# Four more seven-product units in a split-fp32 encoder kernel on one Trainium2 core

## The chip, the cores and the metric

The kernel runs on one core of one Trainium2 chip. The metric is the device time of one execution in microseconds (us), the median of several runs. The engines' names are those of the profile: PE is the matrix engine (matmuls), PEld its weight load, DVE the vector engine, ACT the scalar engine, POOL the GpSimd engine, SP the queue that issues the weight loads from the chip's memory.

## The reference, cut to what matters

Two layers of an encoder over 256 tokens of width 2048, all in fp32. Layer 0 mixes tokens by neighbourhood attention (16 heads of 128, one output projection of 2048 by 2048), layer 1 by a gated short convolution (an input projection to 6144, a three-tap convolution, an output projection of 2048 by 2048). Each layer is followed by a gated feed-forward block: an up-projection to 2 x 5632 columns, a three-tap convolution over positions, silu of one half times the other, and a down-projection back to 2048.

```python
h = h + mixed                                   # mixed = attention or short convolution, @ w_o / w_out
h = h + conv_glu_ffn(rms_norm(h, ffn_norm[i]), ffn_w_up[i], ffn_conv_w[i], ffn_conv_b[i], ffn_w_down[i])

def conv_glu_ffn(x, w_up, conv_w, conv_b, w_down):
    h = dwconv_centered(x @ w_up, conv_w) + conv_b
    g, u = jnp.split(h, 2, axis=-1)
    return (jax.nn.silu(g) * u) @ w_down
```

Each projection streams its weights from the chip's memory while PE works.

## The kernel before, in words

**Split fp32.** PE multiplies in a reduced format, so each fp32 operand x is held as a high part (ACT casts it, line L198 for weights, L318 for activations) and a low part (DVE subtracts, L201 and L319). A product costs three matmuls: high x high, high x low, low x high (function `product`, lines L480 to L482). In the up- and input projections (`Phase`, lines L279 and L287) the same sum is made in another arrangement of the operands.

**Projections back to the model width** are done by the class `Tokens`: the attention's output (called wo here), the four down-projections (two halves of the hidden width in each of two layers), and the convolution mixer's output. Each has two groups g of 1024 output columns. In a group four accumulators 11, 21, 12 and 22 (token half, column half; 128 tokens by 512 columns each, tile `mm`) are summed over pairs of 128-deep contraction blocks. The text of a plan such as `P0 P1 H5 P2 H6 P3 H7 P4` is the order of the pairs.

- A **P** pair has two weight chunks, left and right column half, 128x1024 each. It takes 2 blocks x 4 accumulators x 3 = 24 matmuls of 128x512.
- An **H** pair is done with seven block products in place of eight (`seven`): 7 x 3 = 21 matmuls. Four of the products go to four more accumulators (tile `mu`). It needs sums of weight blocks and sums of activation blocks. For each H pair and group (a "unit") four weight chunks are prepared: left (128x1024), w22 (128x512, split into hi and lo inside one tile), t13 and t42 (128x1024 each). Half of t42 is one more addition on DVE (L160). After the last H of a group, `combine` adds the `mu` accumulators into the residual stream `h`: one ACT copy (L514) and eight DVE operations of 128x512 (L515 to L522). The accumulators `mm` are added to `h` by `residual` (L377).

**Weight sums** are made in memory by DMA, far ahead: `make` issues three 256 KB copies per unit on ACT's DMA queue and three accumulating DMAs on POOL's queue into a buffer `kept`, which SP loads later (512 KB and 256 KB). The tuples QK_JOBS, V_JOBS, UP_JOBS and SC_JOBS say how many such jobs are issued in which earlier projection; the jobs run in the order in which the units are used.

**Activation sums** ("forms") are made by `make_forms`: four POOL operations of 128x128 (through `pool`, L233, which keeps POOL's work in program order), then a split into high (ACT) and low (DVE) parts. In the attention they are made in `mix`, which handles two heads at a time: ACT copies the pair's result out of PSUM (L686, tile `s`, two buffers), POOL makes the four sums in another `s` tile, ACT and DVE split them. `mix` for heads 12 and 13 and for heads 14 and 15 falls into the first items of wo.

**What sets the order.** The program is written item by item; before each item the chunks up to four further ones are loaded and split, `after(n, fn)` puts a function n items later, and a scheduler fixes each engine's order of instructions before the run. Each engine executes its list in order. Tiles come from rings: `raw`, `hi` and `lo` have six buffers each, `s` two, `a` 16 (first the attention's input, then the next layer's input), `act` 22.

At a **seam** (the end of one group and the start of the next) DVE has, in its list, the low parts of the last P pair and of the next group's first pair, `combine`, and the four residual additions. The first item of the next group writes accumulators 11 and then 21 again, six matmuls each, so it needs the old 11 and 21 added to `h` by then.

In the last down-projection the last two pairs are done by `finale`, which closes the accumulators one after the other so that the output can begin.

Of the kernel before, what the change touches and what calls it, by code (L numbers as in the profile page):

```python
# [15 lines left out]
F32 = mybir.dt.float32  # L16
# [6 lines left out]
P = 128  # L23
D = 2048
S = 256
KT = D // P
NH = 16
# [18 lines left out]
def plan(text, due):  # L46


    words = text.split()
    return (tuple(int(x[1:]) for x in words), {int(x[1:]): {"H": 3, "K": 4}[x[0]] for x in words if x[0] != "P"}, due)  # L50


S_FIRST = (plan("P0 H1 H3 H4 H5 P2 H6 H7 H8 H9 P10", 3), plan("P0 H1 H3 H4 H5 P2 H6 H7 H8 H9 P10", 6))
S_SECOND = plan("P0 P2 H1 H3 H4 P9 H5 H6 H7 H8 P10", 0)
S_MLP = {(0, 0): S_FIRST, (0, 1): (plan("P0 H1 H3 H4 H5 P2 H6 H7 H8 H9 P10", 0), plan("P0 P2 H9 H1 H3 H4 H5 H6 H7 H8 P10", 0)),
         (1, 0): S_FIRST, (1, 1): (S_SECOND, plan("P0 P2 H1 H3 H4 P5 H6 H7 H8 P9 P10", 0))}
S_OUT = (plan("P0 H1 H2 P3 H4 H5 H6 P7", 0), plan("P0 P3 H1 H2 H4 H5 H6 P7", 0))
S_ATT = (plan("P0 P1 H5 P2 H6 P3 H7 P4", 0),) * 2
QK_JOBS, V_JOBS, UP_JOBS, SC_JOBS = (0, 2, 2, 2), (2, 2, 2, 2), (12, 13, 11, 13), 14


HEAD = (2, 4)
# [18 lines left out]
def trunk(ctx, tc, xT, par, bias, wqk, wv, wo, wsc, wscout, wup, wdown, out):  # L81
    nc = tc.nc
# [3 lines left out]
    tp = ctx.enter_context(tc.tile_pool(name="tmp", bufs=2))  # L86
# [141 lines left out]
    def pool(op, **of):  # L228

        with ExitStack() as order:  # L230
            if "POOL" in newest:
                order.enter_context(tc.issue_after(newest["POOL"].ins))
            newest["POOL"] = op(**of)  # L233
# [64 lines left out]
    def after(n, fn):  # L298
        later.append((at[0] + n, fn))
# [33 lines left out]
    def a_tile():  # L333
        return ap_.tile([P, 2 * S], F32R, name="a", tag="a", bufs=KT)
# [204 lines left out]
    def make_forms(xe, xo, place, fresh=False):  # L539

        if fresh:
            form_at[:], left_over[:] = ("sf", "vv", "qk") * 2, ()
        v = tp.tile([P, 4, P], F32, name="s", tag="s")
        x11, x21, x12, x22 = (x[:, t * P:(t + 1) * P] for x in (xe, xo) for t in range(2))
        pool(nc.gpsimd.tensor_sub, out=v[:, 0, :], in0=x21, in1=x22)
        pool(nc.gpsimd.tensor_sub, out=v[:, 1, :], in0=v[:, 0, :], in1=x11)
        pool(nc.gpsimd.tensor_add, out=v[:, 3, :], in0=x12, in1=v[:, 1, :])
        pool(nc.gpsimd.tensor_sub, out=v[:, 2, :], in0=x11, in1=x21)
        if isinstance(place, tuple):
            hi, lo = place  # L550
            split_into(hi, lo, v.rearrange("p f c -> p (f c)"))
            return [(hi[:, j * P:(j + 1) * P], lo[:, j * P:(j + 1) * P]) for j in (0, 1, 3, 2)]

        blocks = 3 if place else 4
        y = form_slots(blocks)
        if isinstance(y, list):
            at = [(x[:, :P], x[:, P:]) for x in y]
            to = [(*at[j], v[:, j]) for j in range(blocks)]
        else:
            y = y.rearrange("p (b t c) -> p t b c", t=2, c=P)  # L560
            at = [(y[:, 0, j], y[:, 1, j]) for j in range(blocks)]
            to = [(y[:, 0, :blocks], y[:, 1, :blocks], v[:, :blocks])]
        if place:
            at.append((place[:, P:2 * P], place[:, 3 * P:]))
            to.append((*at[3], v[:, 3]))

        def splits():
            for x in to:
                split_into(*x)
        after(LATE, splits)  # L570
        return [at[j] for j in (0, 1, 3, 2)]
# [30 lines left out]
    oT = [None] * NH  # L602
    oforms = {}
# [66 lines left out]
    def mix(hs, v):  # L670

        o = pa.tile([P, 2, S], F32, name="o", tag="o")
        for i, h in enumerate(hs):
            for k in range(2):
                p = heads[h]["pT"][k]
                vh, vl = (x[:, h % 4 * P:(h % 4 + 1) * P] for x in v[k])
                nc.tensor.matmul(o[:, i, :], lhsT=vh, rhs=p[:, :S], start=k == 0, stop=False)
                nc.tensor.matmul(o[:, i, :], lhsT=vh, rhs=p[:, S:], start=False, stop=False)
                nc.tensor.matmul(o[:, i, :], lhsT=vl, rhs=p[:, :S], start=False, stop=k == 1)
        for i, h in enumerate(hs):  # L680
            oT[h] = act_tile()
            split(oT[h], o[:, i, :])
            heads[h].clear()
        if hs[0] // 2 in S_ATT[0][1]:
            x = tp.tile([P, 2, S], F32, name="s", tag="s")
            nc.scalar.copy(out=x, in_=o)  # L686

            place = tuple((a_tile if hs[0] // 4 == NH // 4 - 1 else act_tile)() for _ in range(2))
            oforms[hs[0] // 2] = make_forms(x[:, 0, :], x[:, 1, :], place)

    class Values:

# [40 lines left out]
    def sc_evac(f, ps):  # L733
# [11 lines left out]
        else:  # L745
# [3 lines left out]
            if j % 2 == 0:  # L749
                sc_of["even"] = t  # L750
            elif j // 2 in S_OUT[0][1]:
                yforms[j // 2] = make_forms(sc_of["even"], t, in_both(S_OUT, j // 2) and yT[j - 1], not yforms)

# [185 lines left out]
    for r in range(KT // STEP):  # L939
        for i in range(STEP // 2):  # L940
            k = r * STEP + 2 * i
# [101 lines left out]
```

## Time and profile before

| what | value |
|---|---|
| median of 3 runs | 2181.46 us (2181.4 to 2182.39) |
| the profiled execution's own time | 2181.86 us |
| its span (first to last instruction) | 2180.1 us |
| PE busy | 2170.2 us (100%), 11681 matmuls |
| DVE busy | 1768.3 us (81%) |
| ACT busy | 1329.0 us (61%) |
| POOL busy | 360.9 us (17%) |
| granted PE clock | 0.998 |
| moved by DMA | 582.61 MB, mean 267 GB/s |

A busy time is the union of an engine's instructions; matmuls overlap one another, so the distance between the starts of matmuls, and not the duration of one, is what a matmul costs. The stage boundaries in the trace: wo runs from 304 to 392 us, the convolution's output from 1373 to 1455 us, the last down-projection from 2055 to 2170 us.

### The profile page before, as it was taken

Reading aid. Unit: us, or ns where it says so; the run is one execution under the profiler, and the core shown is the slowest. Engines: PE = TensorE matmul, PEld = TensorE weight load, DVE = VectorE, ACT = ScalarE, POOL = GpSimd, SP = SyncE. Lnnn points to the kernel's source line nnn. Section 1 sums busy time; section 2 is a strip of 40 time slices with the busy share of each in tenths; the row PEclk is TensorE's granted clock in tenths of the full one; section 3 lists DMA queues with packets and bytes.
Section 4 is the critical chain, followed back from the end, with each engine's and each line's share of the span. In section 5 each row is a group of like instructions: output and inputs, shape, how many; then the busy total and the mean of one; then the engine's idle time right before and its main releaser. Section 6 shows DMA issues by size and latency. Waiting matters only on the chain.

```text
span 2180.1 us, 33378 instructions
## 1 busy us (share of the span) xinstructions
PE 2170.2 (100%) x11681; PEld 1882.8 (86%) x11681; DVE 1768.3 (81%) x2703; ACT 1329.0 (61%) x2032; POOL 360.9 (17%) x410
## 2 busy tenths in 40 slices
PE   9999999999999999999999999999999999999998
PEld 8888888888888888888888888888888888888887
DVE  8777668878789977779986676898788998788798
ACT  7555556665566666666764455666666666566565
POOL 0232130023220013230001323001222000232100
PEclk9999999999999999999999999999999999999999
DMA  8999997799998999999879999787999889999885
GB/s 282 280 280 252 263 222 251 226 278 261 279 262 281 313 257 291 291 258 276 271 241 263 291 302 272 256 270 217 281 288 258 268 286 289 286 269 285 234 273 184
DMA packets 451160, 582.61 MB, mean 267 GB/s; under 512 B 23344, under 2 KB 349616, under 8 KB 450992
## 3 DMA queue, kind: packets, MB, share of 16 engines
q1 hardware_dynamic: 235520, 458.84, 61.4%
q0 software_dynamic: 92400, 60.57, 20.7%
q10 hardware_dynamic: 123072, 61.07, 10.2%
q8 instruction: 92, 1.51, 0.3%
q14 instruction: 76, 0.62, 0.1%
HBM read 578.29 MB, written 123.21 MB: 322 GB/s over the span
## 4 chain that ended last, share of the span: by engine, by line
PE 98%; DVE 1%; ACT 0%; issue 0%; DMA 0%; SPq 0%; ACTq 0%; DVEq 0%
PE mm L279 43%; PE mm L287 22%; PE mm L480 6%; PE mm L481 6%; PE mm L482 6%; PE mu L481 3%; PE mu L480 3%; PE mu L482 3%; PE mm L712 1%; PE mm L713 1%; PE mm L714 1%; PE tr L388 1%; PE tr L665 0%; DMA raw<-in_wqk 0%; DVE lo L201 0%
## 5 line engine op out<-in xcount | busy, mean ns | idle before, releaser
L201 DVE TENSOR_TENSOR lo<-raw,hi 128x1024 fp32r<-128x1024 f32 (+1 forms) x869 | 1032.7, 1214 | 205.3 <-PE mm L287 135.0
L198 ACT CAST hi<-raw 128x1024 fp32r<-128x1024 f32 (+1 forms) x946 | 935.2, 1007 | 415.1 <-PE mm L279 105.1
L279 PE MATMUL mm<-a,hi 128*128 128x512 f32 x4096 | 961.9, 391 | 0.8 <-DVE a L327 0.5
L279 PEld LDWEIGHTS mm<-a,hi 128*128 128x128 f32 x4096 | 759.3, 188 | 154.3 <-DVE a L327 2.4
L287 PEld LDWEIGHTS mm<-a,lo 128*128 128x128 f32 x4096 | 512.9, 191 | 11.8
L287 PE MATMUL mm<-a,lo 128*128 128x256 f32 x4096 | 518.1, 283 | 0.0
L480 PE MATMUL mm<-hi,act 128*128 128x512 f32 x570 | 222.5, 390 | 0.0
L482 PE MATMUL mm<-hi,act 128*128 128x512 f32 x570 | 221.9, 390 | 0.0
L358 DVE SCALAR_TENSOR_TENSOR conv<-pad,pt,conv 128x256 f32<-128x256 f32 x384 | 184.1, 481 | 28.8 <-ACT conv L356 17.9
L233 POOL DMA_DIRECT2D kept<-in_wdown x122 | 163.3, 1918 | 262.0 <-DMA kept<-in_wdown 262.0
L356 ACT ACTIVATE conv<-pad,pt 128x256 f32<-128x256 f32 x176 | 105.7, 602 | 150.8 <-DVE pad L348 150.8
L481 PE MATMUL mm<-lo,act 128*128 128x512 f32 x498 | 194.0, 389 | 0.0
L342 ACT COPY corr<-mm 128x256 f32<-128x256 f32 x256 | 93.8, 370 | 134.9 <-PE mm L287 133.4
L233 POOL TENSOR_TENSOR s<-conv 128x128 f32<-128x128 f32 x62 | 31.5, 508 | 740.4 <-DVE conv L771 740.4
L480 PEld LDWEIGHTS mm<-hi,act 128*128 128x128 f32 x570 | 107.0, 188 | 22.3 <-DVE h L377 0.4
L482 PEld LDWEIGHTS mm<-hi,act 128*128 128x128 f32 x570 | 107.0, 188 | 22.2
L343 DVE TENSOR_TENSOR corr<-mm,corr 128x256 f32<-128x256 f32 x256 | 106.8, 418 | 22.7 <-ACT corr L342 22.7
L233 POOL DMA_DIRECT2D kept<-kept x77 | 80.4, 1047 | 199.0 <-DMA kept<-in_wdown 112.0
L481 PEld LDWEIGHTS mm<-lo,act 128*128 128x128 f32 x498 | 93.5, 188 | 18.8
L319 DVE TENSOR_TENSOR act<-conv,act 128x256 fp32r<-128x256 f32 x88 | 38.5, 438 | 68.3 <-ACT act L318 68.3
L480 PE MATMUL mu<-hi,sf 128*128 128x512 f32 x213 | 82.9, 389 | 0.0
L481 PE MATMUL mu<-lo,sf 128*128 128x512 f32 x213 | 82.9, 389 | 0.0
(160 smaller groups left out, 1723.7 us busy)
## 6 DMA issues: line engine op xcount, KB each, us to landing
raw<-in_wup SPq DMA_DIRECT2D x352, 512.0 KB, 6.4
raw<-in_wdown SPq DMA_DIRECT2D x115, 512.0 KB, 5.0
raw<-in_wsc SPq DMA_DIRECT2D x96, 512.0 KB, 6.8
kept<-in_wdown ACTq DMA_DIRECT2D x183, 256.0 KB, 6.4
raw<-kept SPq DMA_DIRECT2D x77, 512.0 KB, 5.3
kept<-in_wdown POOLq DMA_DIRECT2D x122, 256.0 KB, 12.0
raw<-in_wqk SPq DMA_DIRECT2D x56, 512.0 KB, 6.7
kept<-kept POOLq DMA_DIRECT2D x77, 256.0 KB, 10.6
```

The lines of the kernel that those rows point to most:

```text
L198: newest["ACT"] = nc.scalar.copy(out=hv, in_=r)
L201: newest["DVE"] = nc.vector.tensor_sub(out=lv, in0=r, in1=hv.bitcast(F32))
L233: newest["POOL"] = op(**of)
L279: nc.tensor.matmul(self.ps[ft], lhsT=prepped[i][0][:, o:o + P], rhs=self.src[k], start=k == 0, stop=False)
L287: nc.tensor.matmul(self.ps[ft][:, S:], lhsT=prepped[i][1][:, o:o + P], rhs=self.src[k][:, :S], start=False, stop=k == self.nk - 1)
L342: nc.scalar.copy(out=corr, in_=ps[:, S:])
L343: nc.vector.tensor_add(out=corr, in0=ps[:, :S], in1=corr)
L356: nc.scalar.activation(c, x[:, 1:S + 1], AF.Identity, scale=w[1], bias=b)
L358: nc.vector.scalar_tensor_tensor(out=c, in0=x[:, tap:tap + S], scalar=w[tap], in1=c, op0=ALU.mult, op1=ALU.add)
L480: nc.tensor.matmul(ps, lhsT=xh, rhs=wh, start=start, stop=False)
L481: nc.tensor.matmul(ps, lhsT=xh, rhs=wl, start=False, stop=False)
L482: nc.tensor.matmul(ps, lhsT=xl, rhs=wh, start=False, stop=stop)
```

## The change

Four units more are done with seven products: 81 in place of 77.

- wo: pair 4 becomes an H pair in both groups; the order is P0 P1 H5 P2 H6 H4 H7 P3.
- The convolution's output: pair 3 becomes H in the first group (six H pairs in a row); in the second it stays P.
- The last down-projection, second group: pair 5 becomes H (seven H pairs in a row, in the order of before).
- Pair 4's activation sums are not made from PSUM in its own `mix` but after the last `mix` (heads 14 and 15): two POOL additions of 128x256 restore heads 8 and 9 as high part plus low part, and `make_forms` then runs on these. Its parts lie in two `a` tiles.
- The weight-sum jobs are dealt out anew: 13, 13, 13, 14 in the four up-projections in place of 12, 13, 11, 13. The first of them in the attention now belong to wo's added units.

```diff
-         (1, 0): S_FIRST, (1, 1): (S_SECOND, plan("P0 P2 H1 H3 H4 P5 H6 H7 H8 P9 P10", 0))}
-S_OUT = (plan("P0 H1 H2 P3 H4 H5 H6 P7", 0), plan("P0 P3 H1 H2 H4 H5 H6 P7", 0))
-S_ATT = (plan("P0 P1 H5 P2 H6 P3 H7 P4", 0),) * 2
-QK_JOBS, V_JOBS, UP_JOBS, SC_JOBS = (0, 2, 2, 2), (2, 2, 2, 2), (12, 13, 11, 13), 14
+         (1, 0): S_FIRST, (1, 1): (S_SECOND, plan("P0 P2 H1 H3 H4 H5 H6 H7 H8 P9 P10", 0))}
+S_OUT = (plan("P0 H1 H2 H3 H4 H5 H6 P7", 0), plan("P0 P3 H1 H2 H4 H5 H6 P7", 0))
+S_ATT = (plan("P0 P1 H5 P2 H6 H4 H7 P3", 0),) * 2
+LATE_PAIRS = (4,)
+QK_JOBS, V_JOBS, UP_JOBS, SC_JOBS = (0, 2, 2, 2), (2, 2, 2, 2), (13, 13, 13, 14), 14
...
-        if hs[0] // 2 in S_ATT[0][1]:
+        if hs[0] // 2 in S_ATT[0][1] and hs[0] // 2 not in LATE_PAIRS:
             x = tp.tile([P, 2, S], F32, name="s", tag="s")
             nc.scalar.copy(out=x, in_=o)
 
             place = tuple((a_tile if hs[0] // 4 == NH // 4 - 1 else act_tile)() for _ in range(2))
             oforms[hs[0] // 2] = make_forms(x[:, 0, :], x[:, 1, :], place)
+        if hs[1] == NH - 1:
+            for i in LATE_PAIRS:
+                x = tp.tile([P, 2, S], F32, name="s", tag="s")
+                for k in range(2):
+                    hi, lo = (oT[2 * i + k][:, j:j + S].bitcast(F32) for j in (0, S))
+                    pool(nc.gpsimd.tensor_add, out=x[:, k, :], in0=hi, in1=lo)
+                oforms[i] = make_forms(x[:, 0, :], x[:, 1, :], tuple(a_tile() for _ in range(2)))
```

## The prediction

> **What bounds the kernel now.** I read the page first, then the groups of instructions, then the timelines of PE, DVE, ACT and POOL around wo and at the ends of the groups.
>
> ```profile
> span 2180.1 us, 33378 instructions
> PE 2170.2 (100%) x11681; PEld 1882.8 (86%) x11681; DVE 1768.3 (81%) x2703; ACT 1329.0 (61%) x2032; POOL 360.9 (17%) x410
> PE 98%; DVE 1%; ACT 0%; issue 0%; DMA 0%; SPq 0%; ACTq 0%; DVEq 0%
> L279 PE MATMUL mm<-a,hi 128*128 128x512 f32 x4096 | 961.9, 391 | 0.8 <-DVE a L327 0.5 <-ACT hi L198 0.2
> ```
>
> PE is busy all the time, the chain that ended last is PE's own to 98%, and the most frequent matmul waited 0.8 us in 4096 uses. So whatever takes matmuls away shortens the run by their spacing, as long as the other engines keep up. What a matmul costs is read from starts, not durations. PE's timeline in wo's first group, with the first matmuls of P3, H7 and P4 and two of the next group:
>
> ```profile
> 333.04 0.39 PE L480 MATMUL mm<-hi,act 128*128 128x512 f32 x1
> 338.48 0.39 PE L480 MATMUL mu<-hi,act 128*128 128x512 f32 x1
> 343.24 0.39 PE L480 MATMUL mm<-hi,act 128*128 128x512 f32 x1
> 348.68 0.39 PE L480 MATMUL mm<-hi,act 128*128 128x512 f32 x1
> 350.04 0.39 PE L480 MATMUL mm<-hi,act 128*128 128x512 f32 x1
> ```
>
> The P pair takes 338.48 - 333.04 = 5.44 us for 24 matmuls, the H pair 343.24 - 338.48 = 4.76 us for 21: both 0.227 us each. **An added unit saves 0.68 us of PE, four save 2.72 us.** That is 0.12% of the time; a measurement of this kernel can tell about 0.2% (4.4 us) from no change, so even the full gain lies below that.
>
> **What a unit asks of DVE.** H needs three subtractions of 128x1024, one of 128x512 and one addition; P needs two of 128x1024. DVE's timeline in a group with eight H pairs in a row (second half of layer 0, second group) shows one 128x512 subtraction per H pair; these are the second and the sixth of the row:
>
> ```profile
> 1065.39 0.69 DVE L201 TENSOR_TENSOR hi<-raw,hi 128x512 fp32r<-128x512 f32 x1
> 1085.15 0.68 DVE L201 TENSOR_TENSOR hi<-raw,hi 128x512 fp32r<-128x512 f32 x1
> ```
>
> Four pairs in 19.76 us is 4.94 us of DVE per H pair, against 4.76 us of PE. In a row of H pairs DVE falls behind by 0.18 us per pair. Two subtractions in succession take 2.28 us (lines starting 322.14 and 324.42 below), so a P pair gives DVE 5.44 - 2.28 = 3.16 us to catch up. **Turning P into H adds 4.94 - 2.28 = 2.66 us to DVE and takes 0.68 us from the time it has.** Where that ends late is at the seam: DVE has to run `combine` and the residual additions before PE reuses the accumulators. DVE in wo's first group, with its idle times:
>
> ```profile
> 321.19 0.69 DVE L319 TENSOR_TENSOR a<-s,a 128x512 fp32r<-128x512 f32 x1 [1.42 <-ACT a L318]
> 322.14 2.36 DVE L201 TENSOR_TENSOR lo<-raw,hi 128x1024 fp32r<-128x1024 f32 x2 [0.26 <-ACT hi L198]
> 324.42 0.68 DVE L201 TENSOR_TENSOR hi<-raw,hi 128x512 fp32r<-128x512 f32 x1
> ...
> 329.62 2.59 DVE L201 TENSOR_TENSOR lo<-raw,hi 128x1024 fp32r<-128x1024 f32 x2 [0.17 <-ACT hi L198]
> ...
> 334.52 2.36 DVE L201 TENSOR_TENSOR lo<-raw,hi 128x1024 fp32r<-128x1024 f32 x2 [0.99 <-ACT hi L198]
> 337.09 1.23 DVE L201 TENSOR_TENSOR lo<-raw,hi 128x1024 fp32r<-128x1024 f32 x1 [0.21 <-ACT hi L198]
> 339.81 1.23 DVE L201 TENSOR_TENSOR lo<-raw,hi 128x1024 fp32r<-128x1024 f32 x1 [1.50 <-ACT hi L198]
> ...
> 341.56 2.35 DVE L201 TENSOR_TENSOR lo<-raw,hi 128x1024 fp32r<-128x1024 f32 x2
> 343.83 0.68 DVE L515 TENSOR_TENSOR s<-mu,s 128x512 f32<-128x512 f32 x1
> ...
> 348.63 1.28 DVE L377 TENSOR_TENSOR h<-mm,h 128x512 f32<-128x512 f32 x2
> ```
>
> Idle from 322 us to the seam: 0.26 + 0.17 + 0.99 + 0.21 + 1.50 = 3.13 us. From 339.81 on DVE has no gap, and the second accumulator (the first of the two at 348.63, about 0.68 us long) is free at 349.31; PE writes it from 350.04. The margin is 0.73 us.
>
> **The change, part by part.**
>
> *wo, first group.* DVE gets 2.66 us for H4 and 0.62 us for splitting pair 4's sums (0.68, pipelined), and PE arrives 0.68 us earlier: 3.96 us, against 3.13 us of idle time. That leaves 0.83 us, 0.10 us over the margin. To this comes what POOL does to DVE. Pair 4's sums are two additions of 128x256, which the trace does not show, and four of 128x128. Their rows (minimum, median and maximum, ns), the two chains now run, and DVE's work beside the first of them:
>
> ```profile
> L233 POOL TENSOR_TENSOR bias<-bias,pt x16: 1012/1164/2973, 31.3 to 273.4; 128x384 f32<-128x384 f32 x16
> L233 POOL TENSOR_TENSOR s<-s x12: 452/462/1519, 248.1 to 320.1; 128x128 f32<-128x128 f32 x12
> ```
>
> ```profile
> 311.34 3.03 POOL L233 TENSOR_TENSOR s<-s 128x128 f32<-128x128 f32 x4 [25.40 <-ACT s L686]
> 312.40 1.23 DVE L201 TENSOR_TENSOR lo<-raw,hi 128x1024 fp32r<-128x1024 f32 x1 [1.76 <-ACT hi L198]
> 317.64 2.86 POOL L233 TENSOR_TENSOR s<-s 128x128 f32<-128x128 f32 x4 [3.28 <-ACT s L686]
> 318.54 1.23 DVE L201 TENSOR_TENSOR lo<-raw,hi 128x1024 fp32r<-128x1024 f32 x1 [1.60 <-ACT hi L198]
> 320.45 1.71 POOL L233 DMA_DIRECT2D kept<-kept x2
> ```
>
> A 128x256 addition lies between 0.46 us (128 columns) and 1.01 us (384); I take the middle, 0.73. Four operations of 0.46 would be 1.9 us; with a DVE subtraction beside them they take 3.03 and 2.86, and the longest operation, 1.52 us, is the shortest plus 1.07: POOL stood still while DVE subtracted. What DVE loses to POOL is bounded by nothing from below and by POOL's whole work from above: 2 x 0.73 + 4 x 0.46 = 3.3 us, less the first addition, which falls into DVE's idle 1.42 us before 321.19 (POOL is done with pair 7 at 317.64 + 2.86 = 320.5): 2.6 us. In the four forms above it was POOL that waited, not DVE, so I take the middle, 1.3 us. **The seam then costs 0.1 + 1.3 = 1.4 us, with ends 0.1 and 2.7.**
>
> The Trainium skill has a rule on this: in SBUF — State Buffer, Who interferes with whom, a DVE instruction with two SBUF inputs and a GpSimd instruction that reads SBUF exclude each other for a whole instruction, and whichever starts first keeps the port. The trace agrees, with the 1.52 us. By that rule the two engines' work adds up and the seam would cost up to the 2.7 us; without it 0.1. The same skill, GPSIMD Engine Reference, Elementwise, gives 4497 ns for an addition of 2048 columns, by which an estimate for 256 would be 0.56 us and the upper end 0.3 us lower.
>
> *wo, second group.* The same units without pair 4's sums. DVE is not held up by POOL there and starts the group further ahead; 0.1 us at most, I take 0.
>
> *Convolution output.* Six H in a row in the first group in place of three after a P: 3 x 0.18 = 0.5 us later at the seam. With wo's margin of 0.73 us, which I assume for it, that is 0; the upper end is 0.5. Pair 3's sums and split run in the input projection, under PE, with the five that are there already.
>
> *Last down-projection.* Seven H in a row in place of three after P5: 4 x 0.18 = 0.72 us later at its end, where the margin is small:
>
> ```profile
> 2162.23 1.28 DVE L377 TENSOR_TENSOR h<-mm,h 128x512 f32<-128x512 f32 x2
> 2163.03 0.60 PE L812 MATMUL tr<-pt,h 128*128 128x128 f32 x4
> ```
>
> The first of these additions ends at 2162.91 and PE transposes its result at 2163.03, 0.12 us later; behind the transposes stand PE's remaining matmuls. So 0.72 - 0.12 = 0.6; the ends are 0 (DVE may take the addition before `combine`) and 0.8. **I take 0.5 us.** If the cover were gone altogether, the seven pairs would cost what DVE needs more than PE, 1.3 us.
>
> *Jobs and loads.* Each unit adds three copies on ACT's DMA queue, three accumulating DMAs on POOL's and two loads on SP's:
>
> ```profile
> raw<-in_wup SPq DMA_DIRECT2D x352, 512.0 KB, 6.4
> raw<-in_wv SPq DMA_DIRECT2D x32, 512.0 KB, 4.7
> L198 ACT CAST hi<-raw 128x1024 fp32r<-128x1024 f32 (+1 forms) x946 | 935.2, 1007 | 415.1 <-PE mm L279 105.1 <-PE mm L482 79.8 <-DMA raw<-in_wup 33.1
> ```
>
> ACT waits mostly for PE, that is, for free buffers; its 33.1 us for up-projection weights have reached PE for none. I take 0. If a job held one weight load back by the difference of the medians, 1.7 us, and all of it reached PE, four would cost 6.8 us.
>
> **Sum.** -2.72 + 1.4 + 0.5 = -0.8 us on the profiled execution's 2181.86 us (span 2180.1 and 1.8 around it): 2181.0. The median of the runs is 0.4 us below that execution, so the forecast for the median is 2181.46 - 0.8 = **2180.7 us**.
>
> **The rivals.**
>
> *Everything is hidden.* Chance 0.26. If POOL slips its six operations into DVE's gaps and the last group's addition comes early, only 0.1 us is paid: 2181.46 - 2.72 + 0.1 = 2178.8. For it: 77 units run now with hardly a PE wait. Against it: DVE has no gap from 339.81 to the seam.
>
> *ACT's queue stops behind pair 4's split.* Chance 0.20, the one on the slower side. ACT runs its list in order:
>
> ```profile
> 314.40 0.62 ACT L318 CAST a<-s 128x512 fp32r<-128x512 f32 x1 [2.03 <-POOL s L233]
> 317.46 1.05 ACT L198 CAST hi<-raw 128x1024 fp32r<-128x1024 f32 x1
> 320.54 0.62 ACT L318 CAST a<-s 128x512 fp32r<-128x512 f32 x1 [2.03 <-POOL s L233]
> ```
>
> Both splits stand one weight cast behind the copy and hold ACT for 2.03 us. If pair 4's stands one cast behind pair 7's, ACT waits from 322.1 until POOL is through: 320.5 + 3.3 + DVE's 0.6 and 1.2 between = 325.6. The casts of H6 queue behind it, and DVE behind them. DVE then loses POOL's 2.6 us and 1.1 us more that it waits for the split and the first cast behind it: 0.1 + 3.7 = 3.8 at the seam, with the last group's 0.5: 4.3 - 2.72, 1.6 us slower, 2183.0. It decides from a stall of 2.2 us in wo on. Against it: casts of P2 and H6 may stand ahead of the split.
>
> *The DMA jobs reach PE.* Chance 0.05, 2181.46 - 0.8 + 6.8 = 2187.5. Against it speaks the 0.8 us in 4096.
>
> *Units without gain*, H4's sums so late that the pair itself waits: PE comes to H4 at 333.04 and the sums are there by 328 on the worst count above, so I give it 0.03, with a time like the ACT rival's.
>
> **How the numbers follow.** The forecast has 0.46. Its own range goes from 2179.4 to 2182.0 (seam 0.1 to 2.7). The range of 8 in 10 reaches to the hidden case and to the ACT rival: 2178.6 to 2183.2; left out are the DMA case and the ends. Faster by over 0.2% would need 4.4 us, more than all matmuls saved: 0.03. Slower by over 0.2% is the DMA case or several stalls together: 0.06. Within 0.2%: 0.91.
>
> **What would show it.** In the new profile 12 matmuls fewer; PE's distance between the first matmuls of H4 and H7 4.76 us. In wo's first group DVE without idle time from 322 us to the seam, and PE's first item of the second group, or the transposes behind it, waiting 1 to 2 us for L377. A wait of about 0.5 us at the transposes L812 near the end. ACT's third cast a<-s with a wait of over 2 us and few casts between it and pair 7's would speak for the ACT rival; POOL operations of 0.5 us and DVE idle time left in wo for the hidden case. A fall of more than 3 us, or PE waits in the up-projections, would make the prediction wrong.

## The result, and the profile after

The changed kernel takes 2194.68 us (median of 6 runs, 2191.94 to 2197.93), the kernel before 2181.43 us beside it (6 runs, 2181.22 to 2182.39). The ratio is 1.006 with a 95% interval of 1.005 to 1.007: **slower by 13.25 us**, 0.6%. The prediction was 2180.7 with a range of 2178.6 to 2183.2, so it was wrong in the sign and by more than its range. The profiled execution took 2197.03 us, 2.35 us over the median.

The page after, first the totals, then the shares of the chain of waits, then the group of matmuls that waits most:

```profile
span 2195.3 us, 33461 instructions
...
PE 2172.2 (99%) x11669; PEld 1881.4 (86%) x11669; DVE 1780.8 (81%) x2718; ACT 1329.2 (61%) x2043; POOL 393.9 (18%) x432
...
PE 82%; DVE 7%; DMA 4%; issue 3%; ACT 2%; POOL 1%; ACTq 0%; DVEq 0%; POOLq 0%; SPq 0%
...
L481 PE MATMUL mm<-hi,act 128*128 128x512 f32 x548 | 216.1, 394 | 12.1 <-DVE corr L344 8.5
```

The 12 matmuls are gone (11681 to 11669), as the change says. But the chain that ended last, PE's own to 98% before, now runs through DVE, DMA and ACT for 13% of the span, and the first product of the projections back, which waited for next to nothing before, waits 12.1 us. (Line numbers after are one higher than before in this part of the file.) PE's waits, in us in total, times, longest:

```profile
PE mm L481 <- DVE corr L344: 8.5, 3, 3.4
PE mm L481 <- DVE h L378: 3.4, 3, 1.5
PE tr L820 <- DVE h L378: 0.5, 1, 0.5
```

The prediction looked for the second and third of these rows. The first is new, and the largest. `corr` is a tile of the up-projection: L343 and L344 take its finished accumulators out of PSUM. Three down-projections cannot start because the up-projection before them has not been cleared away. PE's timeline at the start of the first half's down-projection in layer 0:

```profile
643.64 0.39 PE L483 MATMUL mm<-hi,act 128*128 128x512 f32 x1
647.41 0.79 PE L481 MATMUL mm<-hi,act 128*128 128x512 f32 x1 [3.38 <-DVE corr L344]
648.00 0.63 PE L482 MATMUL mm<-lo,act 128*128 128x512 f32 x1
648.43 0.63 PE L483 MATMUL mm<-hi,act 128*128 128x512 f32 x1
648.85 0.63 PE L481 MATMUL mm<-hi,act 128*128 128x512 f32 x1
```

From 643.64 to 647.41 PE starts nothing, and behind that its matmuls start 0.42 to 0.43 us apart in place of 0.227.

I summed, over the whole trace, by how much the distance between two starts exceeds the steady one: 12.2 us before, 29.5 us after, 17.3 us more. The 17.3 less the 2.72 us of matmuls saved is 14.6 us, against 15.2 us between the two spans. By place:

| place | us lost after | predicted |
|---|---|---|
| start of the down-projection, layer 0, first half (644 us) | 5.2 | 0 |
| the same, layer 1, first half (1712 us) | 4.4 | 0 |
| start of the last down-projection (2070 us) | 3.2 | 0 |
| wo, first seam (350 us) | 3.1 | 1.4 |
| convolution output, seam (1421 us) | 0.6 | 0 |
| last transposes (2178 us) | 0.6 | 0.5 |
| within the last down-projection (2127 us) | 0.4 | 0 |

The first three, 12.8 us, are the result. They stand behind the three up-projections whose job counts were raised (12 to 13, 11 to 13, 13 to 14); behind the one that keeps its 13 jobs there is none.

**What those stages look like.** Windows of 160 us in the first up-projection and, before, in the second as well. The columns are window, its length, the busy times of PE, PEld, DVE, ACT and POOL with their instructions, the granted PE clock, the busy share of the DMA engines and GB/s. Before:

```profile
472.00:632.00 160.00, 160.00 (x919) 141.50 (x918) 128.52 (x217) 95.69 (x159) 46.52 (x56) 1.00 1.00 274
791.00:951.00 160.00, 160.00 (x922) 141.64 (x921) 127.53 (x215) 97.31 (x155) 45.16 (x54) 1.00 1.05 280
```

After, the first up-projection, the three stretches around the stall:

```profile
474.00:634.00 160.00, 160.00 (x919) 141.52 (x919) 123.54 (x210) 92.82 (x155) 46.20 (x56) 1.00 1.02 278
641.00:647.00 6.00, 3.03 (x15) 2.19 (x13) 5.59 (x12) 4.37 (x10) 0.00 (x0) 1.00 1.10 299
647.00:651.00 4.00, 3.59 (x9) 2.87 (x10) 3.89 (x10) 1.89 (x3) 0.00 (x0) 0.57 1.00 321
651.00:657.00 6.00, 6.00 (x28) 4.95 (x27) 5.37 (x8) 4.01 (x7) 0.00 (x0) 1.00 0.31 97
```

Two things are to be seen. The DMA share was 1.00 to 1.05 **before** the change too, with PE at 160 us of 160. The share adds up the times of all packets over 16 engines, so it can pass 1, and it does not tell the stages apart: the second line before is the up-projection that keeps its 13 jobs and stays without a stall, at 1.05, and the stalled one after has 1.02. And with one job more the bytes per second hardly rise (274 to 278), while DVE gets through 210 instructions in place of 217 in the same time, 5 us of its work less. That work is not dropped, it is behind: in 641 to 651 DVE is busy 9.5 us of 10 while PE waits and then runs slowly, and the DMA share falls to 0.31 only after that.

What holds DVE back in this stage is ACT, which makes the high parts and issues the job copies between its casts. ACT's timeline at 536 us, and its waits of this kind over the whole execution after the change (total, times, longest):

```profile
535.98 6.74 ACTq L216 DMA_DIRECT2D kept<-in_wdown  x2
542.84 2.00 ACT L199 CAST hi<-raw 128x1024 fp32r<-128x1024 f32 x2 [6.45 <-DMA kept<-in_wdown]
```

```profile
ACT hi L199 <- DMA kept<-in_wdown: 29.2, 5, 6.5
```

Two issues that take 1.31 us elsewhere (1931 us) take 6.74 here: the second copy is issued only when an earlier copy has landed, and the casts stand behind it. DVE is idle for 4.35 us behind this. Before the change the profile has one such wait, 6.2 us at 563 us. The five after it end at 543, 591, 1611, 1657 and 1994 us, all in the three up-projections with a stall and none in the fourth. ACT's waits for the up-projection weights themselves are no longer than before, 32.0 us against 33.1.

SP, whose list holds the weight loads, waits longer for transfers of jobs too (total, times, longest). Before, then after:

```profile
SPq L177 <- DMA kept<-in_wdown: 50.0, 12, 10.6
```

```profile
SPq L178 <- DMA kept<-in_wdown: 105.9, 17, 12.2
```

**wo's seam.** POOL's timeline (the two new additions and the four sums of pair 4), ACT's (the splits of pair 7 and pair 4 and what stands between them) and PE's at the seam:

```profile
317.83 2.86 POOL L234 TENSOR_TENSOR s<-s 128x128 f32<-128x128 f32 x4 [3.27 <-ACT s L687]
320.77 1.90 POOL L234 TENSOR_TENSOR s<-act 128x256 f32<-128x256 f32 x2
322.75 3.68 POOL L234 TENSOR_TENSOR s<-s 128x128 f32<-128x128 f32 x4
```

```profile
320.73 0.62 ACT L319 CAST a<-s 128x512 fp32r<-128x512 f32 x1 [2.02 <-POOL s L234]
321.25 1.99 ACT L199 CAST hi<-raw 128x1024 fp32r<-128x1024 f32 x2
326.46 0.62 ACT L319 CAST a<-s 128x512 fp32r<-128x512 f32 x1 [3.22 <-POOL s L234]
```

```profile
349.96 0.47 PE L481 MATMUL mm<-hi,act 128*128 128x512 f32 x1 [1.49 <-DVE h L378]
...
352.87 0.50 PE L481 MATMUL mm<-hi,act 128*128 128x512 f32 x1 [1.28 <-DVE h L378]
```

POOL needs 1.90 + 3.68 = 5.6 us for pair 4, where the prediction had at most 3.3. ACT has two weight casts between the splits and then stands for 3.22 us: that is the state that the rival on ACT's queue described, with two casts where it had one. The price at the seam is 1.5 + 1.3 us of waiting. DVE's timeline tells what it loses by this:

```profile
322.33 2.82 DVE L202 TENSOR_TENSOR lo<-raw,hi 128x1024 fp32r<-128x1024 f32 x2 [0.26 <-ACT hi L199]
327.11 0.69 DVE L320 TENSOR_TENSOR a<-s,a 128x512 fp32r<-128x512 f32 x1 [1.96 <-ACT a L319]
```

The two subtractions beside POOL took 2.36 us before, so they lose 0.46 us; and then DVE is idle for 1.96 us until ACT has split pair 4's sums.

### The profile page after: what moved, and what is told of

Same layout as the page of the kernel before. It is cut to its first block, busy times and chain, and to the rows that moved or that the text cites. A ratio compares the mean times of both kernels' runs of the same rounds, so it can differ in the third digit from the quotient of the medians.

```text
span 2195.3 us, 33461 instructions
## 1 busy us (share of the span) xinstructions
PE 2172.2 (99%) x11669; PEld 1881.4 (86%) x11669; DVE 1780.8 (81%) x2718; ACT 1329.2 (61%) x2043; POOL 393.9 (18%) x432
## 4 chain that ended last, share of the span: by engine, by line
PE 82%; DVE 7%; DMA 4%; issue 3%; ACT 2%; POOL 1%; ACTq 0%; DVEq 0%; POOLq 0%; SPq 0%
PE mm L280 37%; PE mm L288 19%; PE mm L481 4%; PE mm L483 4%; PE mm L482 4%; DVE lo L202 3%; PE mu L483 2%; PE mu L482 2%; PE mu L481 2%; DMA kept<-in_wdown 1%; ACT hi L199 1%; PE mm L720 1%; PE mm L721 1%; PE mm L722 1%; POOL s L234 1%
## 5 line engine op out<-in xcount | busy, mean ns | idle before, releaser
L280 PE MATMUL mm<-a,hi 128*128 128x512 f32 x4096 | 961.6, 391 | 0.8 <-ACT hi L199 0.5
L280 PEld LDWEIGHTS mm<-a,hi 128*128 128x128 f32 x4096 | 759.4, 188 | 153.8 <-DVE a L328 1.8
L481 PE MATMUL mm<-hi,act 128*128 128x512 f32 x548 | 216.1, 394 | 12.1 <-DVE corr L344 8.5
L234 POOL DMA_DIRECT2D kept<-in_wdown x124 | 169.0, 1959 | 256.1 <-DMA kept<-in_wdown 256.1
L483 PE MATMUL mm<-hi,act 128*128 128x512 f32 x548 | 214.6, 392 | 0.0
L482 PE MATMUL mm<-lo,act 128*128 128x512 f32 x474 | 186.0, 392 | 0.0
L234 POOL TENSOR_TENSOR s<-conv 128x128 f32<-128x128 f32 x62 | 36.2, 583 | 726.2 <-DVE conv L779 726.2
L344 DVE TENSOR_TENSOR corr<-mm,corr 128x256 f32<-128x256 f32 x256 | 106.9, 419 | 60.7 <-ACT corr L343 60.6
L343 ACT COPY corr<-mm 128x256 f32<-128x256 f32 x256 | 91.1, 369 | 96.7 <-PE mm L288 95.9
L481 PEld LDWEIGHTS mm<-hi,act 128*128 128x128 f32 x548 | 103.5, 189 | 36.8 <-DVE corr L344 10.8
L234 POOL DMA_DIRECT2D kept<-kept x81 | 88.1, 1091 | 197.5 <-DMA kept<-in_wdown 103.4
L483 PEld LDWEIGHTS mm<-hi,act 128*128 128x128 f32 x548 | 103.6, 189 | 21.5
```

Of the source, the lines that this page charges most:

```text
L280: nc.tensor.matmul(self.ps[ft], lhsT=prepped[i][0][:, o:o + P], rhs=self.src[k], start=k == 0, stop=False)
L343: nc.scalar.copy(out=corr, in_=ps[:, S:])
L344: nc.vector.tensor_add(out=corr, in0=ps[:, :S], in1=corr)
L481: nc.tensor.matmul(ps, lhsT=xh, rhs=wh, start=start, stop=False)
L482: nc.tensor.matmul(ps, lhsT=xh, rhs=wl, start=False, stop=False)
L483: nc.tensor.matmul(ps, lhsT=xl, rhs=wh, start=False, stop=stop)
```

## The experiments

My theory after the traces: **the jobs of a stage overload the DMA engines**; loads come late, DVE and ACT fall behind, and the stage's end is late. The rivals: **the units themselves** cost the time, pair 4's late sums above all, wherever the jobs are; and **ACT's issuing queue** is what is late, since the job copies stand on it among the casts (Q where an expectation uses a letter). The first four kernels ran beside a kernel before of 2181.5 us.

**The changed kernel with the up-projections' counts of before**, its four extra jobs put into the attention.

```diff
-QK_JOBS, V_JOBS, UP_JOBS, SC_JOBS = (0, 2, 2, 2), (2, 2, 2, 2), (13, 13, 13, 14), 14
+QK_JOBS, V_JOBS, UP_JOBS, SC_JOBS = (0, 3, 3, 3), (3, 2, 2, 2), (12, 13, 11, 13), 14
```

> All 81 units of the change, but the four up-projections issue 12, 13, 11 and 13 weight-sum jobs as before the change; the four jobs more are issued in the attention (18 there in place of 14). Theory J (the jobs added to the up-projections delay weight loads and casts, PE then waits for the last evacuations at the start of the down-projections): the three stalls at the first items of the down-projections (5.2, 4.4 and 3.1 us in the changed kernel's profile) go, 2183 to 2184 us. Rival U (the added units themselves, or the order that the scheduler gives the whole program, make the stalls): they stay, 2192 to 2196 us.

Measured: 2189.26 us (5 runs), ratio 1.0034 (1.0021 to 1.0047). PE's waits:

```profile
PE o L678 <- DVE act L320: 3.8, 2, 2.5
...
PE mm L481 <- DVE h L378: 2.9, 3, 1.4
```

All three `corr` waits are gone. In their place PE waits 3.8 us in the attention (L678), in the stages that were given the jobs; in large part for that the time missed the expected 2184 us. ACT stands at three copies for 4.42 and 5.85 us (at 86 and 162 us) shortly before the two waits. The cost went with the jobs, and the seam in wo stayed.

**The kernel before, its 77 units, with 13 jobs in each up-projection.**

```diff
-QK_JOBS, V_JOBS, UP_JOBS, SC_JOBS = (0, 2, 2, 2), (2, 2, 2, 2), (12, 13, 11, 13), 14
+QK_JOBS, V_JOBS, UP_JOBS, SC_JOBS = (0, 1, 2, 1), (2, 2, 2, 2), (13, 13, 13, 13), 13
```

> The 77 units of before, but 13 jobs in each of the four up-projections (before: 12, 13, 11, 13), two fewer in the attention and one fewer in the convolution's input projection. Theory J: PE waits some 3 to 5 us at the start of the down-projections behind the two up-projections with more jobs, none behind the two with 13 as before: 2186 to 2191 us. Rival U: no stall, 2181 to 2182 us.

Measured: 2189.66 us (6 runs), ratio 1.0036 (1.0023 to 1.0049).

```profile
PE mm L480 <- DVE corr L343: 4.5, 2, 2.8
```

Two `corr` waits, at 641 and 1706 us, the two stages with 13 jobs in place of 12 and 11; none behind the others. No unit was added and no sum made late, and 8 us are lost. For these stalls the units are acquitted: three jobs moved from one place to another are enough.

**As the first, but pair 4 uses pair 7's activation sums**, so that its own two additions, four sums and split are left out.

```diff
-                x = tp.tile([P, 2, S], F32, name="s", tag="s")
-                for k in range(2):
-                    hi, lo = (oT[2 * i + k][:, j:j + S].bitcast(F32) for j in (0, S))
-                    pool(nc.gpsimd.tensor_add, out=x[:, k, :], in0=hi, in1=lo)
-                oforms[i] = make_forms(x[:, 0, :], x[:, 1, :], tuple(a_tile() for _ in range(2)))
+                oforms[i] = oforms[7]
```

> As the run with the jobs moved into the attention, but pair 4's activation sums are left out: the pair uses pair 7's sums in their place, so its two POOL additions, four POOL sums and the split are not there. Theory D (the 3 us at wo's seam are DVE's work for H4 plus what the late sums take from DVE and ACT): without the sums the seam costs 0 to 0.5 us, 2.5 to 3 us less than with them, 2180 to 2181 us. Rival H (the seven-product pair alone fills DVE): the seam still costs 2 to 3 us, 2183 us.

Measured: 2184.88 us (10 runs), ratio 1.0018 (1.0008 to 1.0027). In PE's waits there is no row for wo's seam any more, and the attention's remains, which the expected 2180 to 2181 us had left out:

```profile
PE o L678 <- DVE act L320: 3.0, 2, 2.3
```

**The late sums kept, but pair 4 an H pair in the second group only** (80 units).

```diff
-S_ATT = (plan("P0 P1 H5 P2 H6 H4 H7 P3", 0),) * 2
-QK_JOBS, V_JOBS, UP_JOBS, SC_JOBS = (0, 2, 2, 2), (2, 2, 2, 2), (13, 13, 13, 14), 14
+S_ATT = (plan("P0 P1 H5 P2 H6 P3 H7 P4", 0), plan("P0 P1 H5 P2 H6 H4 H7 P3", 0))
+QK_JOBS, V_JOBS, UP_JOBS, SC_JOBS = (0, 3, 3, 2), (3, 2, 2, 2), (12, 13, 11, 13), 14
```

> 80 units: pair 4 is done with eight products in wo's first group and with seven in the second; its sums are made late as in the change, and the jobs stand as in the run with the jobs moved into the attention. Theory D: DVE has 2.7 us more room in the first group, the seam costs 0 to 0.5 us, one unit (0.7 us) is given back: 2180.5 to 2181.5 us. Rival (ACT's wait for the late sums alone stalls PE): 2 us or more stay in wo, 2183 us.

Measured: 2188.39 us (10 runs), ratio 1.0029 (1.002 to 1.0039); the attention's waits stay (these, too, the expectation had left out), and wo's first seam has none:

```profile
PE o L678 <- DVE act L320: 4.2, 2, 2.4
```

The third and fourth together: either part alone, the H pair in the first group or the late sums, leaves wo's first seam without a wait. It takes both. With the late sums alone (the fourth) DVE still stands 1.97 us for the split, and the seam bears it. That is what a margin looks like: only the sum of the two exceeds what DVE has free.

The next four ran beside a kernel before of 2181.6 us, all with the changed kernel's 81 units but for the last.

**The copies of `make` issued on POOL's queue, or on SP's**, in place of ACT's. This is the test of the queue.

```diff
-            with tc.issue_after(newest["ACT"].ins):
-                nc.scalar.dma_start(out=to, in_=x)
+            pool(nc.gpsimd.dma_start, out=to, in_=x)
```

```diff
-            with tc.issue_after(newest["ACT"].ins):
-                nc.scalar.dma_start(out=to, in_=x)
+            with tc.issue_after(newest["SP"].ins):
+                nc.sync.dma_start(out=to, in_=x)
```

> The changed kernel with all its jobs where they are; only the three 256 KB copies of each job are issued on POOL's queue in place of ACT's. The same bytes move. Theory Q (ACT and SP stand still because a DMA issue waits until an earlier slow copy has landed: both issue in order and share eight completion semaphores, POOL has its own): the stalls at the start of the down-projections go, 2182 to 2185 us with wo's 3 us left. Rival B (the DMA engines have no bandwidth left for the added jobs, whoever issues them): the stalls stay, 2192 us or more.

> The changed kernel, the copies issued on SP's queue in place of ACT's. Theory Q in the form that ACT's standing still is what counts (its casts queue behind the blocked issue): ACT is free, the stalls shrink to under half, 2184 to 2188 us. Form in which the delayed weight loads count: SP now carries all of it, the stalls are as large or larger, 2193 us or more.

Measured: 2214.09 us on POOL's queue (4 runs; 1.0148, 1.013 to 1.0167) and 2208.39 us on SP's (4 runs; 1.012, 1.0105 to 1.0135). Both are worse than the changed kernel by 14 to 19 us. ACT's wait for up-projection weights in the changed kernel, the same with the copies on POOL, and PE's waits with the copies on SP:

```profile
ACT hi L199 <- DMA raw<-in_wup: 32.0, 34, 2.1
```

```profile
ACT hi L199 <- DMA raw<-in_wup: 74.6, 81, 2.6
```

```profile
PE mm L481 <- DVE corr L344: 13.2, 4, 5.3
```

ACT no longer issues a copy, has no wait for one, and waits 74.6 us for weights where it waited 32.0. The queue theory falls as the whole account: with ACT's queue free of the copies the stalls stay, now with ACT late for want of weights. ACT's standing at the copies is the way that the changed kernel's traces show, not the only one by which the jobs can cost time. The Trainium skill says in DMA: Bandwidth & Descriptors, Issuing engines are not separate DMA queues, that transfers run on the same 16 DMA engines whichever engine issues them; both runs agree, in that no queue made room. Why the other two queues are worse than ACT's was not tried.

**The same 81 units and the same counts, spread over more items.** A stage's jobs are issued evenly over the items named in `hosts`.

```diff
-                  jobs=take(UP_JOBS[2 * layer + half]), hosts=(1, 20) if half else (8, 25))
+                  jobs=take(UP_JOBS[2 * layer + half]), hosts=(1, 21) if half else (6, 25))
```

> The changed kernel with the same 13, 13, 13, 14 jobs, spread over 19 items in place of 17 in the first and third up-projection and over 20 in place of 19 in the fourth: 0.68, 0.68, 0.68 and 0.70 jobs per item; before the change 0.71, 0.68, 0.65, 0.68. Theory J with the rate of jobs as its measure: the three stalls go or shrink to under 1 us each, 2184 to 2187 us. Rival (the number of jobs in a stage counts, not the rate): 2192 us or more.

Measured: 2183.53 us (10 runs), ratio 1.0008 (0.9998 to 1.0017). The `corr` row is gone, and 11.2 us with it. PE's waits, the window that answers to those above, and SP's waits for the jobs' transfers:

```profile
PE mm L481 <- DVE h L378: 2.0, 2, 1.3
...
PE tr L820 <- DVE h L378: 0.9, 1, 0.9
```

```profile
473.00:633.00 160.00, 160.00 (x918) 141.49 (x918) 127.72 (x220) 97.81 (x159) 44.30 (x56) 1.00 1.03 276
```

```profile
SPq L178 <- DMA kept<-in_wdown: 45.6, 13, 9.2
```

Nothing was taken out: the same bytes, the same units, the same stages. Only the jobs per item fell, from 13/17 = 0.76 and 14/19 = 0.74 to 0.68 and 0.70 (in the second up-projection from 0.68 to 0.65); before it was 12/17 = 0.71 at most. The DMA share is as high as ever (1.03), but DVE gets its 220 instructions done, SP waits 45.6 us for the jobs' transfers in place of 105.9, and ACT has no wait for an `in_wdown` copy. The time is even a little under the expected 2184 us. Here the rate of the jobs, not their number, makes the difference.

**80 units at an even rate**: the plans of the fourth kernel with these counts.

```diff
+QK_JOBS, V_JOBS, UP_JOBS, SC_JOBS = (0, 2, 2, 2), (2, 2, 2, 2), (13, 13, 13, 13), 14
+                  jobs=take(UP_JOBS[2 * layer + half]), hosts=(1, 20) if half else (6, 25))
```

> 80 units (pair 4 with eight products in wo's first group), 14 jobs in the attention as before the change, 13 in each up-projection, 14 in the convolution's, spread over 19 items in the first and third up-projection. Theories J and D together: neither the stalls behind the up-projections nor those in the attention nor wo's, 0.5 us each left at the convolution's seam and at the end: 2180 to 2181.5 us. Otherwise 2184 us or more.

Measured: 2180.93 us (10 runs), ratio 0.9997 (0.9988 to 1.0007). With neither overloaded stage nor late first seam, 0.7 us of the three units' 2.04 are left, which the interval does not tell from nothing. The 0.9 us below are 0.20 at wo's first seam and 0.74 at the convolution's.

```profile
PE mm L481 <- DVE h L378: 0.9, 2, 0.7
...
PE tr L820 <- DVE h L378: 0.5, 1, 0.5
```

What remains unclear after these is which part of a job loads the engines, and whether the rate alone stalls the kernel before. Two more kernels ask that, beside a kernel before of 2181.5 us (where their expectations say B, the load of the DMA engines is meant).

**The kernel before with its jobs over fewer items** (12 and 11 jobs over 15 items in place of 17), nothing else.

```diff
-                  jobs=take(UP_JOBS[2 * layer + half]), hosts=(1, 20) if half else (8, 25))
+                  jobs=take(UP_JOBS[2 * layer + half]), hosts=(1, 20) if half else (10, 25))
```

> The kernel before, unit for unit and job for job; only the 12 and 11 jobs of the first and third up-projection are issued over 15 items in place of 17 (0.80 and 0.73 per item in place of 0.71 and 0.65), with the same last item. If the rate of jobs is the cause: PE waits 2 to 5 us behind the first up-projection and 0 to 3 behind the third, 2184 to 2188 us. Rival (the changed plans, the scheduler's new order or the number of jobs make the stalls): 2181.5 us.

Measured: 2185.5 us (10 runs), ratio 1.0019 (1.001 to 1.0029). PE's waits and its timeline:

```profile
PE mm L480 <- DVE corr L343: 1.8, 1, 1.8
```

```profile
1704.47 0.39 PE L482 MATMUL mm<-hi,act 128*128 128x512 f32 x1
1706.65 0.50 PE L480 MATMUL mm<-hi,act 128*128 128x512 f32 x1 [1.79 <-DVE corr L343]
```

The rate alone (the jobs also begin two items later) makes the kernel before slower by 4 us, with the same stall in the same place. It is no clean threshold, though: the profiled execution has the stall behind layer 1's first half, with 11/15 = 0.73 jobs per item, and none behind layer 0's, with 0.80. ACT stands at the copies in both: 6.11 and 6.17 us in the stage that stalls, 5.87 and 4.37 in the one that does not.

**The changed kernel without the accumulating DMAs**, the copies all issued as they are, so that the weight sums are not formed.

```diff
-        steps[key] = [lambda: (add(t1, r0), add(t3, r0)), lambda: add(t2, t1)] + [lambda: add(t4[0], t2)] * len(t4)
+        steps[key] = []
```

> The changed kernel, all jobs' copies issued as they are, but the accumulating DMAs on POOL's queue are left out, so the weight sums are not formed (a fifth of the DMA engines' time in the profile). Theory B (the DMA engines' total work): the weight loads and copies land early, no stall behind the up-projections, only wo's 2 to 3 us and the end's 0.6: 2181 to 2184 us. Theory Q (the issues on ACT and SP, which are all still there, are what stalls): stalls of several us stay, 2188 us or more.

Measured: 2183.46 us (10 runs), ratio 1.0008 (0.9999 to 1.0018).

```profile
474.00:634.00 160.00, 160.00 (x918) 141.47 (x917) 128.93 (x220) 97.67 (x159) 13.87 (x28) 1.00 0.76 235
```

Same counts as the changed kernel, same hosts, the same copies on ACT's queue: no `corr` wait, DVE back at 220 instructions, DMA share 0.76. With the half of `make` that runs on POOL's queue gone, the copies land sooner (4.6 us in the median in place of 7.7), ACT has no wait for one any more, and the stalls go; the kernel ends where the wider hosts end, at 2183.5 us, which keep every accumulating DMA. So the issues on ACT's queue do not stall by themselves, only when the transfers before them are slow. That POOL's issuing slows DVE's instructions is not what is seen: they take 0.588 us in the mean in the stalled stage and 0.586 here (busy time over count in the windows). What fits these runs is the sum of the transfers in a stretch of time. Whether a copy taken away would do as much as an accumulating DMA was not tried.

**One added unit at a time**, each with 12, 13, 12, 13 jobs and those of the first halves over items 6 to 25, beside a kernel before of 2181.54 us (33 runs):

```diff
+QK_JOBS, V_JOBS, UP_JOBS, SC_JOBS = (0, 2, 2, 2), (2, 2, 2, 2), (12, 13, 12, 13), 14
+                  jobs=take(UP_JOBS[2 * layer + half]), hosts=(1, 20) if half else (6, 25))
...
+         (1, 0): S_FIRST, (1, 1): (S_SECOND, plan("P0 P2 H1 H3 H4 H5 H6 H7 H8 P9 P10", 0))}
...
+S_OUT = (plan("P0 H1 H2 H3 H4 H5 H6 P7", 0), plan("P0 P3 H1 H2 H4 H5 H6 P7", 0))
...
+S_ATT = (plan("P0 P1 H5 P2 H6 P3 H7 P4", 0), plan("P0 P1 H5 P2 H6 H4 H7 P3", 0))
```

The first two lines are common; of the three plans each kernel has one: the last down-projection's, the convolution output's, wo's second group with the late sums.

> The kernel before with one unit more, pair 5 of the last down-projection's second group, and one job more in the third up-projection (jobs of the first and third spread over 19 items). Theory D: PE saves 0.7 us and pays 0.5 to 1 us at the transposes near the end, where the addition they need comes late: 2181.2 to 2181.9 us, no gain. Rival (the wait at the end is hidden): 2180.8 us.

> The kernel before with one unit more, pair 3 of the convolution output's first group, and one job more in the third up-projection (spread over 19 items). Theory D: PE saves 0.7 us and pays 0.4 to 0.9 us at the seam after six seven-product pairs in a row: 2181.2 to 2181.7 us. Rival (the row of six is hidden, as the prediction had it): 2180.8 us.

> The kernel before with one unit more, pair 4 in the second group of the attention's output, its sums made late as in the change; jobs of the first and third up-projection spread over 19 items. Theory D: the pair itself has cover (0.7 us saved), the late sums cost up to 0.4 us at the first group's seam: 2180.8 to 2181.2 us. Rival (the late sums cost as much in the first group without H4): 2182 us or more.

| unit | median of 11 runs | ratio and interval | predicted for its part |
|---|---|---|---|
| last down-projection | 2181.17 us | 0.9998 (0.9989 to 1.0007) | -0.68 + 0.5 |
| convolution output | 2181.14 us | 0.9998 (0.9989 to 1.0007) | -0.68 |
| wo, second group | 2180.46 us | 0.9994 (0.9985 to 1.0003) | -0.68 |

None can be told from no change. The profile of the first has the wait that the prediction gave it (shown below). PE's waits of the other two have no row for their seams, so the 0.4 to 0.9 us that the second expectation put there and the up to 0.4 us of the third were not paid in these executions:

```profile
PE tr L812 <- DVE h L377: 0.5, 1, 0.5
```

**The two units that cost nothing at their seams, together** (79 units; the plans of wo's second group and of the convolution output, jobs 13, 13, 13, 12 over the same items).

> 79 units: pair 4 in the second group of the attention's output and pair 3 in the first of the convolution's; the last down-projection as before; jobs 14 in the attention, 13, 13, 13, 12 and 14. Theory: 1.4 us saved, 0.4 and 0.4 to 0.9 us paid at two seams: 2180.8 to 2181.5 us. If the best of the added units are free: 2180.1 us.

Measured: 2180.18 us (11 runs), ratio 0.9995 (0.9986 to 1.0003), the lowest median of all. That is 1.36 us less than before, twice 0.68, and close to the expectation's second case, 2180.1. Beside two waits that all these kernels have elsewhere (L115, L838), PE's waits are down to these:

```profile
PE mm L280 <- ACT hi L199: 0.4, 1, 0.4
PE mm L280 <- DVE a L328: 0.2, 1, 0.2
```

The interval still includes 1, so this is no kernel shown to beat the one before; the size fits the matmuls saved, and no more is claimed.

## Why the prediction was wrong

**The step that failed is "Jobs and loads ... I take 0".** The step argued that ACT waits mostly for PE and that the up-projections' matmuls had lost 0.8 us in 4096. Both rows are right and neither says what it was used for: they show that nobody was late, not that there was room. ACT does not wait for buffers and weights alone: it also stands at its own copies, and these waits (for `in_wdown`) went from 6.2 to 29.2 us. The DMA share of the stages that get the jobs, 1.00 to 1.05 already, was the warning. On the page it is the line of the DMA slices, full of eights and nines; I read past it because PE did not wait. The changed kernel with wider hosts and the one without accumulating DMAs agree at 2183.5 us, so the jobs cost 2194.68 - 2183.5 = **11.2 us** of the median.

**The rival "the DMA jobs reach PE" had the right place and too small a price and chance.** It had 0.05 and 6.8 us, one load late by 1.7 us per job. The loss is made otherwise, as the traces show it: ACT stands some 6 us at a time at a copy, DVE falls some 5 us behind (210 for 217 instructions in 160 us), PE works on, which fits chunks that are prepared up to four items ahead, and the debt falls due at the end of the stage, when the accumulators have to be cleared for the next projection. So no up-projection matmul waited: the row of L280 still shows 0.8 us in all, as before. The prediction's sign to look for, "PE waits in the up-projections", was one stage early.

**wo, first group.** Predicted 1.4 us between 0.1 and 2.7; measured 3.1 in the profiled execution of the changed kernel and 2.0 us of waiting in the two kernels without job stalls. The place, the waiting line and the waiting instruction were as said, and that both the H pair and the late sums are needed is shown. Mis-sized was the term for POOL, 1.3 us. Pair 4's POOL work was put at 3.3 us and took 5.6: the two 128x256 additions 0.95 us each in place of 0.73, the four small ones 3.68 in place of 1.84. But DVE lost only 0.46 us directly to it; the larger part is the 1.96 us that DVE stood for the split, the wait that the prediction had only in its rival on ACT's queue, with 1.1 us. With the prediction's own 0.1 that is 0.1 + 0.46 + 1.96 = 2.5 us, against 2.35 us of late starts in the kernel with wider hosts, which has the same two numbers. The 3.1 us of the changed kernel have one more wait of DVE in them, 0.69 us for a cast (346 us). By the prediction's own mark, a stall of 2.2 us in wo, this part went the rival's way. That the seam came near the upper end that the rule of the Trainium skill (SBUF — State Buffer, Who interferes with whom) gave, 2.7 us, is therefore luck: by that rule DVE would have lost POOL's work itself. The prediction's estimate of 0.56 us for an addition would have lowered that end by 0.2 us, not 0.3, since only one of the two additions is in it.

**wo, second group**: 0, as said; no wait there in any kernel, and the kernel with that unit alone is 1.08 us below the one before, within its interval. **Convolution seam**: 0 predicted, upper end 0.5; 0.6 us in the changed kernel (row below), 0.74 in the 80 units at an even rate, none with wider hosts, in the kernel with that unit alone or in the 79 units; what decides there was not tried. **Last down-projection**: 0.5 predicted, 0.46 of waiting measured (0.89 with wider hosts):

```profile
1421.52 0.50 PE L481 MATMUL mm<-hi,act 128*128 128x512 f32 x1 [0.61 <-DVE h L378]
...
2178.38 0.66 PE L820 MATMUL tr<-pt,h 128*128 128x128 f32 x4 [0.46 <-DVE h L378]
```

**The matmuls**: 2.72 us, as said. With them the sum closes where the jobs are out of the way: in the profiled execution with wider hosts the starts lose 2.35 us at wo's seam and 1.05 at the end, and 2181.86 (the profiled execution before) - 2.72 + 3.4 = 2182.5, against 2182.34 measured. Its median is 1.2 us higher; by what is not shown. So even without job stalls these four units win nothing: the two late places take 3.4 us of lost starts and give 2.72 of matmuls.

**What stays open.** That the jobs cost the time, and that their rate and the accumulating DMAs' load matter, is shown by runs; that the cost reaches PE through ACT's standing at the copies is read from the traces, and the runs with the copies on other queues show that it is not the only way. Whether the limit lies in the DMA engines or in the memory behind them is not shown. Nor is the threshold: 0.71 jobs per item ran without stalls and 0.73 to 0.76 with them, but the run with 0.80 had none in that stage. The spread may belong to this: the changed kernel's runs lie 6 us apart, those of the kernel before about 1, which would fit a stage that just does or does not catch up.

## What to carry to other kernels

Before work is added that brings transfers, read the DMA share of the very stages that get them, and look at the engine that issues them: what stands behind an issue in its list, and how long does the issue take? A share about 1.00 with no engine waiting is a warning and no more (stages at 1.05 ran without a stall); what told the stalled stages of the changed kernel apart was copies whose issue took some 6 us in place of 1.3. The cost then comes out as a stall at the end of the stage, in another instruction than the one that is late. If the work must be added, spread it evenly over the items first: the same 81 units cost 11 us less when one or two items more carried the jobs. And where a margin at a seam is below a microsecond, add up all the engines' work and waits on the way to it, since here two parts that were each free were not free together.

## What the runs showed of the hardware that I had not expected

**A wait of PE of under 2 us can be followed by matmuls at half pace.** Behind the 3.4 us wait at 644 us the matmuls start 0.42 to 0.43 us apart, and the granted clock in 647 to 651 us is 0.57; from 651 it is 1.00 again. Of the 5.2 us lost there, 3.5 are the gap (3.77 less one spacing) and the other 1.7 are this. Windows of the kernel before with narrower hosts, on both sides of its wait of 1.79 us:

```profile
1702.00:1705.00 3.00, 2.86 (x13) 2.02 (x12) 2.96 (x6) 2.29 (x5) 0.00 (x0) 1.00 1.12 283
1705.00:1709.00 4.00, 2.35 (x7) 1.73 (x8) 3.97 (x8) 0.98 (x4) 0.00 (x0) 0.82 0.94 326
```

Here too the clock falls, to 0.82 in the mean of the window. It does not follow every time: behind the changed kernel's wait of 2.55 us at 2072 us the granted clock stays at 1.00, and behind the waits of 1.3 to 1.5 us at wo's seam the spacing is back at 0.22 to 0.24 from the second start on. The Trainium skill (TensorE: Matmul & The Clock Gate, Part 1: The HAM clock gate) gives half rate after at least one idle window of about 3.4 us, free-running; the half rate agrees, the length does not: 1.79 us was enough in this run.

**The choice of the issuing queue mattered, but not as expected.** The same copies cost 14 us more from SP's queue and 19 us more from POOL's than from ACT's, which has the casts to do besides.
